# Transposing attention's probabilities, mLSTM rows and keys from copies of the rounded 32-bit type

## The chip, the cores and the metric

The kernel runs on one core of a Trainium2 chip. The time is device microseconds of one launch. The engines are named TensorE (PE in the profile, PEld for its weight loads), VectorE (DVE), ScalarE (ACT), GpSimd (POOL) and SyncE (SP, which issues nearly all DMAs).

## The reference

One layer of a hybrid backbone over 1024 latent tokens and 256 context tokens, model width 1024. Cut to what matters here:

```python
u = modulate(rmsnorm(x)) @ w_in          # split: mLSTM q,k,v,o; gates; attention q,k,v
y_m = mlstm_merge(mlstm_bidirectional(...))                 # 4 heads x 128 -> 512 columns
# attention: 8 query heads, 2 key heads, width 64, window 128, all context keys, a sink per head
s_band = einsum('bnqhgd,bnkhd->bnhgqk', qb, kb)             # masked to |i-j| <= 128
s_ctx  = einsum('bnqhgd,bchd->bnhgqc', qb, k_ctx)
p = softmax(concatenate([s_band, s_ctx, s_sink], -1))
y_a = einsum('bnhgqk,bnkhd->bnqhgd', p[band], vb) + einsum('bnhgqc,bchd->bnqhgd', p[ctx], v_ctx)
x = x + g_a * (concatenate([y_m, y_a], -1) @ w_out)
x = x + g_f * conv_glu(modulate(rmsnorm(x)))                # d_ff 2816
return rmsnorm(x) * final_norm
```

## The kernel before

Tokens lie on the 128 partitions in blocks: 2 of context, 8 of latents. Large products are made in a rounded 32-bit type (F32R, fp32r in the profile): an operand is split into a rounded part ("hi", on ScalarE) and the remainder ("lo", on VectorE), and three products are added in PSUM (`mm3`: hi*hi, hi*lo, lo*hi, lines 307 to 309).

The stages in order of time: modulation and input projection, the four mLSTM heads (to about 350 us), the query projection (to about 398 us), attention together with the first half of the output projection (to about 580 us), its second half with the norm of the mixer, the channel mixer's up product, its down product with the final norm. All that is changed lies in the query projection and attention.

In the query projection (`qgen`, `qproj`, `qtrans`) 16 query blocks are projected; each is rounded, transposed (L878, from tiles of the rounded type with the rounded identity `identr`), copied out of PSUM by ScalarE into `QTo` (L880) and stored by SP to `q_d` in HBM (L881). Between them `kprep` loads the keys of a token block (`kb`), transposes them per key head (L852) and splits them into `kT2`.

In attention a *pair* is two query heads of one query block; there are 32 pairs, four for each of the 8 blocks. A loop over steps `t` is a software pipeline: in step t pair t (`A`) gets its scores and exponentials, pair t-1 (`B`) is scaled, pair t-2 (`C`) is transposed and split, pair t-3 (`E`) finishes its product with the values; `N` is the pair after `A`. The scores of a head lie in PSUM (`sps`); `mxo` is the row maximum on VectorE (L1128), `ex` the exponential on ScalarE with the row sum in `ss` (L1132), `nrm` the reciprocal on VectorE (L1136) and the scaling in place on GpSimd (L1139). `tr(i)` transposes two key blocks of both heads from `p_` into PSUM (L1151): 512 keys make 8 transposes and 640 keys 10 for a pair, in blocks of four, four and two. `hi` (ScalarE, L1158) and `lo` (VectorE, L1164) split what comes out, and `pv` (L1174) multiplies with the values into `u`.

`Wout(b, 0)` is the mLSTM half of the output projection of block b: `load` fetches x, `tr` transposes the mLSTM rows from `ym` (L1061), `hi` and `lo` split (L1074, L1078), `mm` multiplies (L307 to L309) and `add` adds to x (L1089). Its pieces are put between those of the pairs by the table `more`, which is keyed by step and slot; block 0 (`w0`) is written into step 0 by hand.

On TensorE, VectorE, ScalarE and GpSimd the order in attention is the order in which the code is written. SP's order is made by a scheduler. Each engine and SP's queue take their instructions in order, and a DMA that waits holds up the DMAs behind it on SP.

Of the kernel before, what the change touches and what calls it, by code (L numbers as in the profile page):

```python
# [9 lines left out]
F32 = mybir.dt.float32  # L10
F32R = mybir.dt.float32r
BF16 = mybir.dt.bfloat16
AF = mybir.ActivationFunctionType
ALU = mybir.AluOpType
# [4 lines left out]
P = 128  # L19
# [10 lines left out]
KVH = 2  # L30
ADH = 64
# [47 lines left out]
def build(tc, I, out, dbg=None):  # L79
    nc = tc.nc  # L80
    dbg = dbg or {}
    V, S, G, T = nc.vector, nc.scalar, nc.gpsimd, nc.tensor
# [3 lines left out]
    ident = cp.tile([P, P], F32, name="ident")  # L86
    identr = cp.tile([P, P], F32R, name="identr")
# [24 lines left out]
    kv_d = kvp.tile([NCH, P, 2 * P], F32, name="kv_d")  # L112
# [11 lines left out]
    ym = rp.tile([P, NL, 512], F32, name="ym")  # L124
# [57 lines left out]
    xp = p1.enter_context(tc.tile_pool(name="xp", bufs=2))  # L182
# [660 lines left out]
        return row_d[8 * i:8 * i + 8, :].rearrange("(o a) b -> o (a b)", o=1).broadcast_to([P, D])  # L843

    def kprep(c):
        kb = xp.tile([P, KVH, 2, ADH], F32, name="kb", tag="kv", bufs=3)
        for i in range(2):
            nc.sync.dma_start(kb[:, :, i], kv_d[c][:, 0:P].rearrange("p (g e) -> p g e", g=KVH))
        yield
        pt = pO.tile([P, 512], F32, name="po", tag="o") if c % 2 else pU.tile([P, 2 * P], F32, name="u", tag="u")  # L850
        for g in range(KVH):
            T.transpose(pt[:, g * P:(g + 1) * P], kb[:, g].rearrange("p a e -> p (a e)"), ident[:])  # L852
        pv = pt[:, 0:256].rearrange("p (g s) -> p g s", g=KVH)
        hi, lo = (kT2[i][:, :, c * P:(c + 1) * P] for i in range(2))
        S.copy(hi, pv)
        V.tensor_tensor(out=lo, in0=pv, in1=hi.bitcast(F32), op=ALU.subtract)
# [61 lines left out]
    def load_q(b):  # L918
        QTs[b] = wm.tile([P, AH, P], F32R, name="QT", tag="QT", bufs=2)
        return nc.sync.dma_start(QTs[b][:].bitcast(F32), q_d[b]).ins  # L920
# [51 lines left out]
    for h in range(H):  # L972
# [20 lines left out]
        with tc.manual_schedule(engines=order_):  # L993
            dn = dense(h + 1, wkq, wvo, *nh) if nh else qgen()
            rate = RATE if nh else RATE3
            for n, _ in enumerate(mlstm(h, *cur)):
# [4 lines left out]
                if nh and n in (2, LW):  # L1001
                    w = wnext((n // LW,))
# [10 lines left out]
                while debt > 0:  # L1013
                    w = next(dn, None)
# [36 lines left out]
    t2 = pa_.enter_context(tc.tile_pool(name="t2", bufs=2))  # L1051


    class Wout:
        def __init__(self, b, attn):
            self.b, self.attn, self.k0, self.po = b, attn, 4 * attn, None

        def tr(self):
            self.po = pO.tile([P, 512], F32, name="po", tag="o")
            for j in range(4):  # L1060
                T.transpose(self.po[:, j * P:(j + 1) * P], ym[:, self.b, j * P:(j + 1) * P], ident[:])  # L1061

        def load(self):
            b = self.b
            self.xb = t3.tile([P, D], F32, name="x2", tag="x2") if self.attn else x2t()
            if self.attn:
                xs[b] = self.xb[:]
            nc.sync.dma_start(self.xb[:], x2_d[b][:] if self.attn else I["x"][b * P:(b + 1) * P, :])

        def hi(self):  # L1070
            self.h, self.l = (t2.tile([P, 512], F32R, name=n, tag=n, bufs=1) for n in ("ymh", "yml"))
            r = lambda a: a[:].rearrange("p (j q) -> p j q", j=4)
            self.src = yTa[:, :, self.b * P:self.b * P + P] if self.attn else r(self.po)
            S.copy(r(self.h), self.src)  # L1074
# [18 lines left out]
    class Pair:  # L1093
        def __init__(self, b, g, r):
            self.b, self.g, self.r = b, g, r
            self.lb, self.hb = max(b - 1, 0), min(b + 1, NL - 1)
            self.nb = self.hb - self.lb + 1
            self.nk = CTX + self.nb * P
            self.nkb = 2 + self.nb
            self.h0 = 4 * g + 2 * r  # L1100
            self.nm, self.ss = (t2.tile([P, 2], F32, name=n, tag=n, bufs=4) for n in ("nm2", "ss"))
            self.sps, self.p, self.sv, self.pt, self.ph, self.pl = [None] * 2, [None] * 2, [None] * 2, [None] * 3, [None] * 3, [None] * 3


        def sk(self, j):
# [26 lines left out]
            S.activation(self.p[j][:, :self.nk + 1], self.sv[j], AF.Exp, bias=self.nm[:, j:j + 1], scale=1.0,  # L1132
                         accum_out=self.ss[:, j:j + 1])

        def nrm(self):
            V.reciprocal(self.ss[:], self.ss[:])  # L1136
            for j in range(2):
                w = slice(0, self.nk)
                G.tensor_scalar(out=self.p[j][:, w], in0=self.p[j][:, w], scalar1=self.ss[:, j:j + 1],  # L1139
                                scalar2=1.0, op0=ALU.mult, op1=ALU.mult)  # L1140

        def kr(self, i):
            return range(2 * i, min(2 * i + 2, self.nkb))
# [1 line left out]
        def tr(self, i):  # L1145
            if not self.kr(i):
                return
            self.pt[i] = pT.tile([P, 512], F32, name="pt", tag="l")
            for kk, kb in enumerate(self.kr(i)):
                for j in range(2):  # L1150
                    T.transpose(self.pt[i][:, (2 * kk + j) * P:(2 * kk + j + 1) * P], self.p[j][:, kb * P:(kb + 1) * P],  # L1151
                                ident[:])

        def hi(self, i):
            w = len(self.kr(i)) * 2 * P
# [44 lines left out]
    more = collections.defaultdict(list)  # L1200

    def token(w, t):
        more[t, 1] += [w.load, w.tr]
        more[t, 2] += [w.hi]
        more[t + 1, 3] += [w.lo]
        tail_of(w, t)
# [33 lines left out]
    for t in range(n + 2):  # L1240
        blk, sub = divmod(t, 4)
        if sub == 0 and blk + 1 < NL:
            lq = load_q(blk + 1)
        if t in WOT:
            k = 4 + WOT.index(t)
            room = [wop.tile([P, D], F32R, name=f"wo{n}{k}")[:] for n in "hl"]
            with tc.issue_after(lq):
                wogs.append(load_wo(k, lambda room=room: room, G, True))
                next(wogs[-1])
        if t + 1 < len(pairs):  # L1250
            live[t + 1] = Pair(*pairs[t + 1])
        N, A, B, C, E = (live.get(t + 1 - i, null) for i in range(5))
        A.S(0)
        E.lo(2)
        B.nrm()
        fill(t, 3)
        rows_step()
        if t == 0:
            next(qpend.pop(0), 0)
            w0.tr()  # L1260
            pdk.close()
            pSs.append((pa_.enter_context(tc.tile_pool(name="pS", bufs=1, space=PSUM, side="right")), "s"))
            live[0].sk(1)
            w0.hi()
            live[0].S(1)
            w0.lo()
        E.pv(1)
        C.tr(0)
        E.pv(2)
        A.mxo(0)  # L1270
        C.hi(0)
        E.y1()
        A.ex(0)
        N.sk(0)
        C.lo(0)
        E.y2()
        fill(t, 0)
        if t == 0:
            for q in qpend:
                next(q, 0)  # L1280
        C.tr(1)
        if t:
            A.S(1)
        C.hi(1)
        A.mxo(1)
        fill(t, 1)
        C.tr(2)
        C.lo(1)
        A.ex(1)
        N.sk(1)  # L1290
        C.hi(2)
        fill(t, 2)
        C.pv(0)
        live.pop(t - 3, None)
# [253 lines left out]
    def wsplit(R, n, eng=V):  # L1548
# [29 lines left out]
                                                                    tag={"a": "a", "f": "b", "b": "b"}.get(n, "c"))  # L1578
# [105 lines left out]
    B = Block(0, None, None)  # L1684
# [21 lines left out]
    for i in range(1, NF):  # L1706
# [12 lines left out]
        if i == 1:  # L1719
# [21 lines left out]
            B = C  # L1741
# [35 lines left out]
        B = C  # L1777
# [5 lines left out]
    g = ExitStack()  # L1783
# [92 lines left out]
    more = {}  # L1876
# [87 lines left out]
    for t, (p, ps, fresh) in enumerate(products):  # L1964
        for j in range(NP):
# [35 lines left out]
            if NP + 3 <= n < NP + 3 + NL:  # L2001
                b = n - NP - 3
# [118 lines left out]
```

## Time and profile before

| | |
|---|---|
| median of 3 runs | 1279.54 us (1278.59 to 1282.48) |
| the profiled execution | span 1281.0 us from the first to the last instruction; the list of times does not say which of the three it is |
| TensorE busy | 1240.8 us, 97% |
| VectorE, ScalarE, GpSimd busy | 974.5, 638.1, 208.8 us |
| mean granted TensorE clock | 0.996 |
| DMA | 175.63 MB, 137 GB/s |

How to read the rows: a timeline row is the start in us, the duration, the engine, the line, the operation, the tiles out and in, the form, and in brackets how long the engine had been idle and what ended that. A row of the windows view is the stretch, then busy time and instructions of PE, PEld, DVE, ACT and POOL, the granted clock, the DMA engines' busy share and GB/s. With a filter by line it holds the engines that this line uses. A row of the DMA view is the transfer, the queue, how many, KB of each and the median time from issue to landing. A matmul's duration reaches from its start to the modelled end of its results, so matmuls in a row overlap.

### The profile page before, as it was taken

Reading aid. Unit: us, or ns where it says so; the run is one execution under the profiler, and the core shown is the slowest. Engines: PE = TensorE matmul, PEld = TensorE weight load, DVE = VectorE, ACT = ScalarE, POOL = GpSimd, SP = SyncE. Lnnn points to the kernel's source line nnn. Section 1 sums busy time; section 2 is a strip of 40 time slices with the busy share of each in tenths; the row PEclk is TensorE's granted clock in tenths of the full one; section 3 lists DMA queues with packets and bytes.
Section 4 is the critical chain, followed back from the end, with each engine's and each line's share of the span. In section 5 each row is a group of like instructions: output and inputs, shape, how many; then the busy total and the mean of one; then the engine's idle time right before and its main releaser. Section 6 shows DMA issues by size and latency. Waiting matters only on the chain.

```text
span 1281.0 us, 19212 instructions
## 1 busy us (share of the span) xinstructions
PE 1240.8 (97%) x7023; PEld 1060.6 (83%) x7023; DVE 974.5 (76%) x1679; ACT 638.1 (50%) x1308; POOL 208.8 (16%) x175
## 2 busy tenths in 40 slices
PE   6999999999999999999899999999999999999997
PEld 4799898999898888887677888888888888788886
DVE  5863687877887878776898777777777776867887
ACT  6632556464865777776644333333333334444435
POOL 1200000000001433232402311332321332001000
PEclk9999999999999999999999999999999999999999
DMA  9431544452254332103413222233222337975563
GB/s 361 180 122 35 141 137 143 123 168 77 84 183 162 134 116 67 67 34 132 135 63 110 105 99 95 104 119 108 101 100 99 106 108 261 345 264 172 194 199 135
DMA packets 90416, 175.63 MB, mean 137 GB/s; under 512 B 12938, under 2 KB 29522, under 8 KB 90322
## 3 DMA queue, kind: packets, MB, share of 16 engines
q1 hardware_dynamic: 90034, 173.63, 40.2%
q8 instruction: 55, 0.90, 0.3%
q10 hardware_dynamic: 288, 0.79, 0.2%
q14 instruction: 39, 0.32, 0.1%
HBM read 136.05 MB, written 38.33 MB: 136 GB/s over the span
## 4 chain that ended last, share of the span: by engine, by line
PE 78%; DVE 8%; ACT 5%; DMA 5%; issue 3%; POOL 1%; SPq 0%; DVEq 0%; ACTq 0%; POOLq 0%
PE pd L1958 14%; PE pa L1450 9%; PE pc L1450 9%; PE pp L588 6%; PE pe L1450 4%; PE pb L1450 4%; PE pd L1450 4%; PE u L1174 3%; PE pt L1151 2%; PE po L307 2%; PE pv L307 2%; PE pv L309 2%; PE pv L308 2%; PE po L309 2%; PE po L308 2%
## 5 line engine op out<-in xcount | busy, mean ns | idle before, releaser
L1552 ACT CAST wh<-Rb 128x1024 fp32r<-128x1024 f32 (+1 forms) x66 | 59.5, 903 | 147.7 <-PE pd L1450 83.0
L1958 PE MATMUL pd<-dh,al 128*128 128x512 f32 x296 | 115.4, 390 | 0.7 <-DVE al L1324 0.6
L1958 PE MATMUL pd<-dl,ah 128*128 128x512 f32 x296 | 115.2, 389 | 0.0
L1958 PE MATMUL pd<-dh,ah 128*128 128x512 f32 x296 | 115.2, 389 | 0.0
L1450 PE MATMUL pc<-hB,wh 128*128 128x512 f32 x344 | 107.1, 393 | 2.5 <-DVE av L1529 2.5
L1450 PE MATMUL pa<-hB,wh 128*128 128x512 f32 x336 | 103.6, 390 | 0.0
L1340 DVE TENSOR_TENSOR wl<-Rb,wh 128x1024 fp32r<-128x1024 f32 (+1 forms) x66 | 68.9, 1045 | 39.4 <-ACT wh L1552 38.8
L1660 POOL TENSOR_TENSOR tt<-vt,tt 128x512 f32<-128x512 f32 x22 | 29.5, 1341 | 325.6 <-ACT tt L1654 325.6
L588 PE MATMUL pp<-hl,wh 128*128 128x512 f32 x256 | 79.3, 405 | 0.0
L1450 PEld LDWEIGHTS pc<-hB,wh 128*128 128x128 f32 x344 | 65.3, 190 | 16.6 <-DVE av L1529 2.9
L307 PE MATMUL pv<-wh,hl 128*128 128x256 f32 x256 | 76.1, 297 | 0.5 <-ACT ym L601 0.5
L1450 PEld LDWEIGHTS pa<-hB,wh 128*128 128x128 f32 x336 | 63.2, 188 | 13.6 <-ACT sn L1624 0.4
L309 PE MATMUL pv<-wh,hl 128*128 128x256 f32 x256 | 72.3, 283 | 0.0
L308 PE MATMUL pv<-wl,hl 128*128 128x256 f32 x256 | 72.3, 282 | 0.0
L1450 PE MATMUL pc<-hB,wl 128*128 128x512 f32 x172 | 67.6, 393 | 0.0
L1958 PEld LDWEIGHTS pd<-dh,al 128*128 128x128 f32 x296 | 55.5, 188 | 12.8 <-DVE al L1324 1.4
L1958 PEld LDWEIGHTS pd<-dl,ah 128*128 128x128 f32 x296 | 55.6, 188 | 11.9 <-DVE dl L1324 0.3
L1450 PE MATMUL pa<-hB,wl 128*128 128x512 f32 x168 | 65.4, 389 | 0.0
L1958 PEld LDWEIGHTS pd<-dh,ah 128*128 128x128 f32 x296 | 55.6, 188 | 11.5
L1158 ACT CAST ph<-pt 128x512 fp32r<-128x512 f32 (+1 forms) x88 | 46.2, 525 | 27.0 <-PE pt L1151 26.8
L1139 POOL TENSOR_SCALAR p__4966<-p__4966,ss 128x512 f32<-128x512 f32 x1 | 0.7, 688 | 346.6 <-DVE ss L1136 346.6
L1450 PE MATMUL pe<-hB,wh 128*128 128x512 f32 x176 | 54.6, 390 | 0.4 <-DVE hB L1340 0.2
(1072 smaller groups left out, 3760.2 us busy)
## 6 DMA issues: line engine op xcount, KB each, us to landing
w<-in_w_ada_dram SPq DMA_DIRECT2D x64, 256.0 KB, 2.7
br<-in_w_down_dram SPq DMA_DIRECT2D x25, 512.0 KB, 6.6
Ra<-in_w_up_dram SPq DMA_DIRECT2D x22, 512.0 KB, 3.6
Rb<-in_w_up_dram SPq DMA_DIRECT2D x22, 512.0 KB, 3.5
ar<-act_s SPq DMA_DIRECT2D x44, 256.0 KB, 3.6
act_a<-tt SPq DMA_DIRECT2D x33, 256.0 KB, 2.0
act_s<-tt SPq DMA_DIRECT2D x33, 256.0 KB, 2.0
wr<-in_w_h_dram SPq DMA_DIRECT2D x16, 512.0 KB, 4.4
```

The costliest lines, as they stand in the source:

```text
L307: T.matmul(ps, st_hi, mv_hi, start=first, stop=False)
L308: T.matmul(ps, st_hi, mv_lo, start=False, stop=False)
L309: T.matmul(ps, st_lo, mv_hi, start=False, stop=last)
L588: T.matmul(pp[:, 512 * n:512 * n + 512], wkq[sw][:, kt, cs], hl[n][part][:, kt, :], start=kt == 0 and sw + part == 0, stop=kt == KT - 1 an ...
L1151: T.transpose(self.pt[i][:, (2 * kk + j) * P:(2 * kk + j + 1) * P], self.p[j][:, kb * P:(kb + 1) * P], ident[:])
L1158: S.copy(self.ph[i][:, :w], self.pt[i][:, :w])
L1174: T.matmul(self.u[:], vv[:, c, self.g], part[i][:, kk * 2 * P:(kk + 1) * 2 * P], start=kb + m == 0, stop=kb == last and m == 1)
L1340: sub = lambda e, o, x, y: e.tensor_tensor(out=o, in0=x, in1=y, op=ALU.subtract)
L1450: T.matmul(ps[:], wt[sw][:, j, ks], hB[part][:, blk, kt, :], start=first and kt == 0 and sw + part == 0, stop=last and kt == 3 and sw == 1 ...
L1552: S.copy(wt[0][:], src)
L1660: G.tensor_tensor(out=self.tt[:, h2_], in0=self.vt[:], in1=self.tt[:, h2_], op=ALU.mult)
L1958: T.matmul(ps[:], ac[sa][:, js], w[sw], start=first and n == 0, stop=last and n == 2, skip_group_check=not fresh)
```

## The change

Three kinds of transposes take their input from a tile of type F32R, with the rounded identity, and write a PSUM tile that is viewed as F32R. The input tile is filled by a DMA whose destination is viewed as plain F32, so the bits are those of the plain numbers.

- Keys: `kb` is of type F32R; the loads that filled it before now fill it under a view as F32.
- mLSTM rows: `Wout.load` also copies the block's rows from `ym` (SBUF) into a new tile `ymb` (SBUF, 256 KB, two buffers), and `tr` reads that. In `token` the load of a block moves from slot 1 of step t, just ahead of its transposes, to slot 2 of step t-1.
- Probabilities: `nrm` takes one head at a time. After the scaling a DMA on SP copies the head's probabilities from `p_` into a new tile `pq_` (256 or 320 KB, five buffers), and `tr` reads that. The first head's `nrm` comes behind its pair's second exponential (`A.nrm(0)`), the second's where both were (`B.nrm(1)`).

```diff
-        kb = xp.tile([P, KVH, 2, ADH], F32, name="kb", tag="kv", bufs=3)
+        kb = xp.tile([P, KVH, 2, ADH], F32R, name="kb", tag="kv", bufs=3)
         for i in range(2):
-            nc.sync.dma_start(kb[:, :, i], kv_d[c][:, 0:P].rearrange("p (g e) -> p g e", g=KVH))
+            nc.sync.dma_start(kb[:, :, i].bitcast(F32), kv_d[c][:, 0:P].rearrange("p (g e) -> p g e", g=KVH))
...
-            T.transpose(pt[:, g * P:(g + 1) * P], kb[:, g].rearrange("p a e -> p (a e)"), ident[:])
+            T.transpose(pt[:, g * P:(g + 1) * P].bitcast(F32R), kb[:, g].rearrange("p a e -> p (a e)"), identr[:])
...
-                T.transpose(self.po[:, j * P:(j + 1) * P], ym[:, self.b, j * P:(j + 1) * P], ident[:])
+                T.transpose(self.po[:, j * P:(j + 1) * P].bitcast(F32R), self.yb[:, j * P:(j + 1) * P], identr[:])
...
+            if not self.attn:
+                self.yb = t2.tile([P, 512], F32R, name="ymb", tag="ymb", bufs=2)
+                nc.sync.dma_start(self.yb[:].bitcast(F32), ym[:, b])
...
-        def nrm(self):
-            V.reciprocal(self.ss[:], self.ss[:])
-            for j in range(2):
-                w = slice(0, self.nk)
-                G.tensor_scalar(out=self.p[j][:, w], in0=self.p[j][:, w], scalar1=self.ss[:, j:j + 1],
-                                scalar2=1.0, op0=ALU.mult, op1=ALU.mult)
+        def nrm(self, j):
+            w = slice(0, self.nk)
+            V.reciprocal(self.ss[:, j:j + 1], self.ss[:, j:j + 1])
+            G.tensor_scalar(out=self.p[j][:, w], in0=self.p[j][:, w], scalar1=self.ss[:, j:j + 1],
+                            scalar2=1.0, op0=ALU.mult, op1=ALU.mult)
+            self.q[j] = t2.tile([P, 640], F32R, name="pq_", tag="pq_", bufs=5)
+            nc.sync.dma_start(self.q[j][:, w].bitcast(F32), self.p[j][:, w])
...
-                    T.transpose(self.pt[i][:, (2 * kk + j) * P:(2 * kk + j + 1) * P], self.p[j][:, kb * P:(kb + 1) * P],
-                                ident[:])
+                    T.transpose(self.pt[i][:, (2 * kk + j) * P:(2 * kk + j + 1) * P].bitcast(F32R),
+                                self.q[j][:, kb * P:(kb + 1) * P], identr[:])
...
     def token(w, t):
-        more[t, 1] += [w.load, w.tr]
+        more[t - 1, 2] += [w.load]
+        more[t, 1] += [w.tr]
...
         E.lo(2)
-        B.nrm()
+        B.nrm(1)
...
         A.ex(1)
+        A.nrm(0)
```

SP's order at the border of the query projection and attention, before. `QT` is the load of a query block, `q_d<-QTo` the stores of the query projection, the first `x` the load of `w0`, the second that of block 1.

```order
L920 DMA QT<-q_d 128x1024
L881 DMA q_d<-QTo 128x512 x3
L1068 DMA x_4926<-in_x_dram 128x1024
L881 DMA q_d<-QTo 128x512 x2
L1068 DMA x_5074<-in_x_dram 128x1024
L881 DMA q_d<-QTo 128x512
L1091 DMA x_d_75<-x_4926 128x1024
```

The same place after the change (lines behind the edits are counted on by 3 to 6).

```order
L920 DMA QT<-q_d 128x1024
L881 DMA q_d<-QTo 128x512 x3
L1068 DMA x_4926<-in_x_dram 128x1024
L881 DMA q_d<-QTo 128x512
L1071 DMA ymb<-ym 128x512
L881 DMA q_d<-QTo 128x512
L1068 DMA x_5048<-in_x_dram 128x1024
L1071 DMA ymb<-ym 128x512 x2
L881 DMA q_d<-QTo 128x512
L1144 DMA pq__4999<-p__4968 128x512
L1144 DMA pq__5019<-p__4995 128x512
L1094 DMA x_d_75<-x_4926 128x1024
```

`w0`'s copy of the mLSTM rows stands behind its x and the fourth of the six stores; on TensorE its transposes keep their place, right behind the last-but-one block of query transposes.

VectorE around the border of two steps in the middle (the row maximum and the reciprocals are those of pair 6), before: `nm` is the row maximum, `pl` a remainder, `yTa` the attention output, `yml` the remainder of the mLSTM rows.

```order
L1128 TENSOR_REDUCE nm_5233<-sps 128x1
L1164 TENSOR_TENSOR pl__5372<-pt,ph 128x512
L1164 TENSOR_TENSOR pl__5396<-pt,ph 128x256
L1136 RECIPROCAL ss<-ss 128x2
L1078 TENSOR_TENSOR yml<-po,ymh 128x512
```

And after:

```order
L1131 TENSOR_REDUCE nm_5261<-sps 128x1
L1168 TENSOR_TENSOR pl__5408<-pt,ph 128x512
L1140 RECIPROCAL ss<-ss 128x1
L1168 TENSOR_TENSOR pl__5436<-pt,ph 128x256
L1140 RECIPROCAL ss<-ss 128x1
L1081 TENSOR_TENSOR yml<-po,ymh 128x512
```

The reciprocal of a pair is split: the first head's stands ahead of the third remainder, the second's where both were. In the first steps, which have no third remainder yet, the two stand next to each other.

The scheduler also moves the load of `er` (the first weights of the channel mixer) on SP from behind a store of x that follows the last query load to behind the query load of block 6, and with it ScalarE's rounding of `er` from ahead of pair 27's first exponential to ahead of pair 20's.

More of the change, by code (lines that the diff above doesn't have):

```diff
@@ L1101, in __init__ @@
             self.nm, self.ss = (t2.tile([P, 2], F32, name=n, tag=n, bufs=4) for n in ("nm2", "ss"))
-            self.sps, self.p, self.sv, self.pt, self.ph, self.pl = [None] * 2, [None] * 2, [None] * 2, [None] * 3, [None] * 3, [None] * 3
+            self.sps, self.p, self.q, self.sv, self.pt, self.ph, self.pl = [None] * 2, [None] * 2, [None] * 2, [None] * 2, [None] * 3, [None] * 3, [None] * 3
         def sk(self, j):
```

## The prediction

> **What bounds the kernel now.** I read the page's first line, then the windows view over the attention stage, where every edit lies, then the TensorE timeline there, and last the queues that the new copies use.
>
> ```profile
> PE 1240.8 (97%) x7023; PEld 1060.6 (83%) x7023; DVE 974.5 (76%) x1679; ACT 638.1 (50%) x1308; POOL 208.8 (16%) x175
> 398.00:414.00 16.00, 14.30 (x95) 12.08 (x95) 9.12 (x19) 9.84 (x28) 3.27 (x5) 1.00 0.45 149
> 414.00:549.00 135.00, 133.44 (x941) 113.51 (x939) 110.63 (x220) 104.08 (x280) 50.85 (x58) 1.00 0.28 98
> 549.00:578.00 29.00, 27.16 (x186) 23.64 (x184) 21.93 (x45) 20.18 (x57) 8.13 (x12) 1.00 0.05 19
> ```
>
> TensorE is occupied for 97% of the span. In the long middle of attention, 414 to 549 us, it is occupied for 133.44 of 135 us at the full clock, with VectorE second at 110.63. So what leaves TensorE there should leave the time, less what new waits take. The first 16 us and the last 29 us are different: there TensorE idles 1.7 and 1.8 us, and a late input moves everything behind it.
>
> **The change part by part. First, the transposes.** Their number comes from the windows view filtered by line, one row each for the probabilities (L1151), the mLSTM rows (L1061) and the keys (L852):
>
> ```profile
> 352.00:585.00 233.00, 47.03 (x304) 36.08 (x304) 1.00 0.31 107
> 352.00:585.00 233.00, 4.87 (x32) 3.36 (x32) 1.00 0.31 107
> 352.00:585.00 233.00, 4.05 (x20) 2.07 (x20) 1.00 0.31 107
> ```
>
> The duration in such a row, about 273 ns, is not the price: matmuls overlap. The price is the time from one start to the next. The kernel already transposes from a tile of the rounded type at one place, the query heads (L878), so both kinds can be read from the timeline. Each pair of pieces below goes from the first transpose of a block to the second 256-wide matmul behind it.
>
> ```profile
> 394.04 0.46 PE L878 MATMUL pt<-identr,qs 128*128 128x128 f32 x4
> 394.33 0.35 PE L307 MATMUL px<-wh,hl 128*128 128x256 f32 x1
> 394.52 0.28 PE L308 MATMUL px<-wl,hl 128*128 128x256 f32 x1
> ...
> 434.87 0.27 PE L1151 MATMUL pt<-ident,p__5260 128*128 128x128 f32 x1
> 434.98 0.27 PE L1151 MATMUL pt<-ident,p__5291 128*128 128x128 f32 x1
> ...
> 435.43 0.28 PE L1118 MATMUL sps<-kT,QT 128*128 128x256 f32 x1
> ```
>
> Four rounded transposes and one 256-wide matmul take 394.52 - 394.04 = 0.48 us; four plain ones and the same matmul take 435.43 - 434.87 = 0.56 us. A block of four saves 0.08 us. It is the first transposes that gain; at the end the matmul behind starts late in both cases.
>
> ```profile
> 358.27 0.89 PE L878 MATMUL pt<-identr,qs 128*128 128x128 f32 x8
> 359.19 0.28 PE L308 MATMUL px<-wl,hl 128*128 128x256 f32 x1
> ...
> 429.42 0.27 PE L1151 MATMUL pt<-ident,p__5193 128*128 128x128 f32 x1
> ...
> 430.41 0.28 PE L1118 MATMUL sps<-kT,QT 128*128 128x256 f32 x1
> ```
>
> A block of eight saves (430.41 - 429.42) - (359.19 - 358.27) = 0.07 us. The 304 of the probabilities stand in 56 blocks of four, 4 of eight and 24 of two; two are nowhere timed in the rounded kind, so between nothing and half a block of four, 0.02 taken: 56 x 0.08 + 4 x 0.07 + 24 x 0.02 = 5.3 us. The mLSTM rows are 8 blocks of four; the first stands in the front of the stage, below, so 7 x 0.08 = 0.6. The keys are 10 blocks of two next to rounded transposes: 0.2. Together at most 6.1 us of TensorE.
>
> How much of it counts? In places TensorE is already waiting for the chain transpose, ScalarE's rounding, VectorE's remainder, product. The idle rows show two such waits in the middle, and the timeline shows small ones as late starts:
>
> ```profile
> PE pt L1151 <- DVE pl__6393 L1164: 0.6, 1, 0.6
> ...
> 434.29 0.36 PE L1174 MATMUL u<-ph,vv 128*128 128x256 f32 x1
> 434.64 0.39 PE L1174 MATMUL u<-pl__5396,vv 128*128 128x256 f32 x1
> ...
> L1136 DVE RECIPROCAL ss<-ss 128x2 f32<-128x2 f32 x32 | 5.0, 157 | 1.4 <-ACT p__4993 L1132 0.8 <-ACT p__7331 L1132 0.2 <-ACT p__5148 L1132 0.2
> ```
>
> At such a place a transpose that ends sooner only lengthens the wait. VectorE, which does the remainder, also gets 32 more reciprocals of up to 157 ns (at most 5.0 us in all), one of them now ahead of the third remainder in every step. It has 24 us free in the middle, so I give them no term, but that cover goes where the remainder is waited for. Of the 6.1 us I take 60%, 3.7; the ends are 0 and 6.1. GpSimd's 64 scalings stay the same in number and size.
>
> **Second, the copies of the mLSTM rows.** Seven of the eight are issued a step ahead. The first cannot be: on SP it now stands behind the query store that waits for ScalarE's rounding of the fourteenth of the sixteen query blocks, while its transposes are the next thing on TensorE.
>
> ```profile
> 397.47 0.33 SPq L1068 DMA_DIRECT2D x<-in_x_dram  x1
> 398.65 0.32 SPq L881 DMA_DIRECT2D q_d<-QTo  x1
> ...
> 398.74 0.62 PE L1061 MATMUL po<-ident,ym 128*128 128x128 f32 x4
> 400.00 0.39 PE L1117 MATMUL sps<-kT,QT 128*128 128x256 f32 x1 [0.64 <-ACT sps L1108]
> 401.24 0.51 PE L307 MATMUL po<-woh,ymh 128*128 128x512 f32 x1 [0.44 <-DVE yml L1078]
> ...
> q_d<-QTo SPq DMA_DIRECT2D x3, 256.0 KB, 2.8
> act_a<-tt SPq DMA_DIRECT2D x33, 256.0 KB, 2.0
> x<-in_x_dram SPq DMA_DIRECT2D x8, 512.0 KB, 3.6
> ```
>
> The store is issued at 398.65 and takes 0.32 to issue, so the copy starts at about 399.0. No row shows a copy inside SBUF. The nearest are the stores of the same 256 KB from SBUF, 2.0 us where the engines are quiet and 2.8 in this window; a 512 KB load takes 3.6, which is the upper end, and nothing excludes a quicker landing than 2.0 but no row has one. With 2.4 it lands at 401.4 instead of being there at 398.74: TensorE's transpose is 2.7 us late. Behind it wait the rounding, the remainder (401.24 follows 398.74 by 2.5 us, all of it chain) and the first output products, and the score matmul at 400.00 with its own 0.64 us of waiting is behind it in order too. VectorE's row maxima stand behind that remainder, so nothing later catches up: +2.7 us, between 2.0 and 4.0.
>
> The Trainium skill, "DMA: Bandwidth & Descriptors", section on the anatomy of one DMA, fits a transfer as a fixed 2.0 us plus its bytes at 436 GB/s, mostly the wait for the write's receipt; it measured GpSimd's path. It speaks against this change, since each new copy would pay that latency whatever its size. By it, as an estimate, 256 KB take 2.6 us and the front is 2.9 us late instead of 2.7; the 2.0 us row for 256 KB is under it.
>
> **Third, the 64 copies of the probabilities.** Each needs GpSimd's scaling before and its transposes after. The old distance is the cover:
>
> ```profile
> 411.13 0.69 POOL L1139 TENSOR_SCALAR p__5033<-p__5033,ss 128x512 f32<-128x512 f32 x1
> 413.71 0.27 PE L1151 MATMUL pt<-ident,p__5033 128*128 128x128 f32 x1
> ...
> 440.17 1.05 POOL L1139 TENSOR_SCALAR p__5421<-p__5421,ss 128x640 f32<-128x640 f32 x1 [2.48 <-DVE ss L1136]
> 444.96 0.27 PE L1151 MATMUL pt<-ident,p__5421 128*128 128x128 f32 x1
> ...
> 563.87 0.69 POOL L1139 TENSOR_SCALAR p__7166<-p__7166,ss 128x512 f32<-128x512 f32 x1 [5.08 <-DVE ss L1136]
> 567.73 0.27 PE L1151 MATMUL pt<-ident,p__7166 128*128 128x128 f32 x1
> ```
>
> From the fifth pair on the first head is scaled in the step before, so the second takes its place on GpSimd: it ends at about 441.2 for a transpose at 444.96, 3.7 us ahead, and at 564.6 for 567.73, 3.2 us ahead, the narrowest. A copy of 2.0 to 2.8 us plus 0.3 for the issue fits. In the first pairs the reciprocals still stand together, and pair 1's second head ends at 411.82 for 413.71: 1.9 us of cover, 0.4 to 1.2 short. Pair 0 is short by 0 to 0.4. I take 0.8 for both. SP is not full: 72 more issues of 0.33 us in 180 us. Behind a copy that waits for GpSimd stand only the loads of later steps. The load of er moves forward, so ScalarE's rounding of it (about 1 us) lands in the step of pair 20 instead of pair 27: 0 to 1 us if er is late, 0.2 taken.
>
> **Sum.** -3.7 + 2.7 + 0.8 + 0.2 = 0.0 against the profiled execution's span of 1281.0 us, which is 1.5 us over the median of the runs. I predict the median unchanged: 1279.5 us. Its own range is -3 to +3, 1276.5 to 1282.5. A measurement of this kernel tells about 0.3%, 3.8 us, from no change.
>
> **Rivals.** *The gain comes whole* (faster): TensorE has no idle in the middle worth naming, which speaks for it; the late starts above speak against. With all 6.1 us and the lower ends of the waits, 2.0 + 0.3: -3.8, or 1275.7; with the front copy hidden too, -5.8, 1273.7. *The copies come late in the middle* (slower): decided when issue plus landing pass 3.2 to 3.8 us, the cover in most steps. The 3.6 us of loads, and loads of 512 KB in the same rings, speak for it; the 2.0 of stores against. At 4.2 us about 20 steps would wait 0.5 us, once each: with the front 1.3 us later still, -3.7 + 4.0 + 0.8 + 0.2 + 10 = +11, 1291. *Nothing is saved in the middle*: between products the loading of the next weights shows, and the chain over ScalarE and VectorE sets the pace. Then 2.7 + 0.8 + 0.2 = +3.7, 1283.2, on the edge of what is told.
>
> **How the numbers follow.** Forecast 0.54, gain whole 0.20, late copies 0.12, nothing saved 0.14. From the second, three quarters are faster by over 0.3%, and a tenth of the forecast: 0.21. From the third nearly all and half of the last are slower, with little of the first: 0.20. Within: 0.59. The range goes from 1274.5, which leaves out a third of the whole gain, to 1284.0, which leaves out the late copies: about 2 in 10 outside.
>
> **What would show it.** L1155's starts 85 ns apart or less inside a block (now 109 or 110); the first L1061 near 401.4 with a DMA as releaser, and no gain before 414; in the windows view 414 to 549 shortened by 3 to 4 us; no rows of PE waiting for pq past the second pair. Wrong would be: pq in the list of waits in every step, er's rounding waited for, or the product rows waiting for the remainder longer by as much as the transposes gave.

## The result and the profile after

The changed kernel is slower: 1287.84 us median of 4 runs (1287.09 to 1290.82) against 1280.66 of the kernel before beside it (1278.59 to 1282.48), a ratio of 1.0064 with a 95% interval of 1.005 to 1.0078. That is 7.2 us more. The forecast was 1279.5, no change, with a range that ended at 1284.0. It was wrong: the kernel is slower than that whole range. The profiled execution took 1287.09 us, with a span of 1285.3. Among all the runs below, one execution (the profiled one of e9) took 2022.66 us at a granted clock of 0.558, and no ratio counts it.

The page of the changed kernel, TensorE's line, and the windows view over the same three stretches as in the prediction (the program runs up to 8.5 us later here):

```profile
PE 1238.9 (96%) x7023; PEld 1057.4 (82%) x7023; DVE 976.2 (76%) x1711; ACT 638.4 (50%) x1308; POOL 210.0 (16%) x175
398.00:414.00 16.00, 11.52 (x51) 9.36 (x51) 4.88 (x10) 5.04 (x15) 1.39 (x2) 0.79 0.53 190
414.00:549.00 135.00, 128.59 (x917) 108.35 (x916) 111.84 (x241) 102.08 (x276) 50.55 (x58) 0.99 0.61 222
549.00:578.00 29.00, 27.63 (x204) 23.98 (x203) 23.37 (x53) 22.50 (x62) 8.04 (x11) 1.00 0.41 158
```

TensorE has as many instructions as before, and is busy 1.9 us less. But in 398 to 414 us it gets through 51 matmuls where it did 95, and the column after the five engines, the granted clock, reads 0.79 where it was 1.00. In the middle the DMA engines are busy 0.61 of the time, against 0.28.

The waits view of TensorE over 396 to 590 us names who ended the idle time. None of the rows for DMA or for `pl__6610` was there before; the two 0.8 rows were 0.6.

```profile
PE po L1061 <- DMA ymb<-ym: 3.9, 1, 3.9
PE pt L1155 <- DMA pq__5044<-p__5022: 1.5, 1, 1.5
...
PE u L1178 <- DVE pl__6610 L1168: 0.9, 1, 0.9
PE pt L1155 <- DMA pq__5440<-p__5410: 0.9, 1, 0.9
PE pt L1155 <- DVE pl__6500 L1168: 0.8, 1, 0.8
...
PE pt L1155 <- DVE pl__5808 L1168: 0.8, 1, 0.8
```

The largest wait on TensorE's timeline, and what comes behind it. The rows are start, duration, engine, line, tiles, and in brackets the idle time:

```profile
397.25 0.52 PE L878 MATMUL pt<-identr,qs 128*128 128x128 f32 x4
401.70 0.72 PE L1061 MATMUL po<-identr,ymb 128*128 128x128 f32 x4 [3.93 <-DMA ymb<-ym]
...
405.26 0.63 PE L307 MATMUL po<-wrm,ymh 128*128 128x512 f32 x1
405.69 0.63 PE L308 MATMUL po<-wrm,ymh 128*128 128x512 f32 x1
...
408.06 0.39 PE L308 MATMUL po<-wrm,ymh 128*128 128x512 f32 x1
408.30 0.39 PE L309 MATMUL po<-wrm,yml 128*128 128x512 f32 x1
```

The wait itself is 3.93 us. Then 512-wide matmuls follow each other at 0.43 us (405.26 to 405.69) where the full clock gives 0.24 (408.06 to 408.30): TensorE came out of the idle time at half its clock, which the trace records from 400.99 to 407.82. The prediction had no such term. The Trainium skill, "TensorE: Matmul & The Clock Gate", section "What's actually happening", says that the clock falls to half after at least one idle window of about 3.4 us. The trace agrees here: the wait is longer than that, and the clock is half behind it. But in some of the runs below a wait of about 2 us was enough, which is shorter than what the Trainium skill states; the runs decide, and e11 has their numbers.

SP's timeline for the copies that were late, and the DMA view's times from issue to landing (last column) for pairs 0 and 1:

```profile
397.52 0.32 SPq L881 DMA_DIRECT2D q_d<-QTo  x1
398.00 0.53 SPq L1071 DMA_DIRECT2D ymb<-ym  x1
...
414.46 0.33 SPq L1094 DMA_DIRECT2D x_d<-x  x1
415.32 0.47 SPq L1144 DMA_DIRECT2D pq__5044<-p__5022  x1
416.00 1.14 SPq L1144 DMA_DIRECT2D pq__5061<-p__5040  x1
```

```profile
pq__4999<-p__4968 SPq DMA_DIRECT2D x1, 256.0 KB, 2.3
...
pq__5044<-p__5022 SPq DMA_DIRECT2D x1, 256.0 KB, 4.2
pq__5061<-p__5040 SPq DMA_DIRECT2D x1, 256.0 KB, 4.2
```

A copy of 256 KB inside SBUF lands after 2.3 us for pair 0. Block 0's rows, issued at 398.00, were used at 401.70: 3.7 us. Pair 1's copies took 4.2.

All the kernels issue the same 7023 matmuls in the same order (e2's 34 extra ones are left out), so the start of each one can be subtracted. The table has what that difference grows by in each stretch of attention (times are those of the kernel before), for the profiled execution of each kernel, in us. "Rest" adds up the three stretches between the named ones. The experiments follow below.

| kernel | front 384.1-413.5 | pair 1 413.5-423.9 | pair 6 439.4-441.2 | er 512.3-512.6 | rest to 573.4 | sum |
|---|---|---|---|---|---|---|
| changed kernel | +5.47 | +3.34 | +0.86 | +1.12 | -2.74 | +8.05 |
| e1 block 0 plain | -0.05 | +3.59 | +1.08 | +1.28 | -2.97 | +2.92 |
| e2 TensorE kept busy | +3.45 | +0.77 | +1.08 | +1.27 | -2.10 | +4.47 |
| e3 block 0, pairs 0, 1 plain | -0.07 | +0.46 | +1.33 | +1.27 | -3.23 | -0.24 |
| e4 no copies | -0.09 | -0.22 | -0.05 | +0.02 | -1.25 | -1.58 |
| e5 er back | +5.11 | +3.38 | +1.26 | +0.01 | -2.86 | +6.90 |
| e6 as e3, er back | -0.10 | +0.75 | +1.11 | +0.02 | -2.82 | -1.04 |
| e7 copies, plain type | +4.35 | +5.30 | +1.23 | +1.19 | -0.69 | +11.38 |
| e8 no copies, er back | -0.09 | -0.24 | -0.05 | +0.04 | -2.72 | -3.07 |
| e9b block 0, pairs 0, 1, 2, 6 plain, er back | -0.02 | +1.02 | +0.02 | +0.05 | -2.63 | -1.55 |
| e10 copy on GpSimd's queue | +7.75 | +3.41 | +1.41 | +1.25 | -3.10 | +10.72 |
| e11 block 0 plain, store moved | -0.09 | +1.75 | -0.05 | +1.22 | -1.24 | +1.58 |

Two differences lie outside these stretches. The query projection ends 0.5 to 1.0 us sooner in 10 of the 12 profiles. Most of it is a wait of 0.62 us for `kb` at 384.11 in the profile of the kernel before; e7, whose keys are plain, lacks that wait too, so it isn't the type's. And the profile of the kernel before loses time of its own at 690 to 705 us:

```profile
696.36 0.73 PE L1450 MATMUL pc<-hB,wh 128*128 128x512 f32 x2 [2.49 <-DVE av L1529]
...
697.44:700.85 3.41, 3.41 (x10) 2.65 (x9) 3.02 (x4) 1.33 (x2) 0.00 (x0) 0.50 0.48 154
```

TensorE waits 2.49 us for `av`, where the changed kernel waits 1.14, and the clock behind it is half. That is 3.0 us, so the two profiled spans differ by 4.3 us only; the 7.2 us are the difference of the medians.

### The profile page after: what moved, and what is told of

The parts are those of the page before. It is cut to its first block, busy times and chain, and to the rows that moved or that the text cites. A ratio compares the mean times of both kernels' runs of the same rounds, so it can differ in the third digit from the quotient of the medians.

```text
span 1285.3 us, 19452 instructions
## 1 busy us (share of the span) xinstructions
PE 1238.9 (96%) x7023; PEld 1057.4 (82%) x7023; DVE 976.2 (76%) x1711; ACT 638.4 (50%) x1308; POOL 210.0 (16%) x175
## 4 chain that ended last, share of the span: by engine, by line
PE 79%; DVE 8%; ACT 5%; DMA 4%; issue 3%; POOL 1%; SPq 0%; DVEq 0%; ACTq 0%; POOLq 0%
PE pd L1964 14%; PE pa L1456 9%; PE pc L1456 8%; PE pp L588 6%; PE pe L1456 4%; PE pb L1456 4%; PE pd L1456 4%; PE po L307 2%; PE u L1178 2%; PE pv L307 2%; PE pv L309 2%; PE pv L308 2%; PE po L309 2%; PE po L308 2%; PE px L309 1%
## 5 line engine op out<-in xcount | busy, mean ns | idle before, releaser
L1131 DVE TENSOR_REDUCE nm<-sps 128x1 f32<-128x641 f32 (+1 forms) x64 | 50.3, 786 | 6.2 <-PE sps L1127 4.7
```

Source lines behind the costliest of these rows:

```text
L1131: V.tensor_reduce(out=self.nm[:, j:j + 1], in_=self.sv[j], axis=AX.X, op=ALU.max, negate=True)
```

## The experiments

Times are medians; each ratio is to the kernel before, run on the same chip (1280.14 to 1280.84 us), with its 95% interval.

**e1: block 0's rows plain.**

```diff
-                T.transpose(self.po[...].bitcast(F32R), self.yb[...], identr[:])
+                if self.b == 0:
+                    T.transpose(self.po[...], ym[:, 0, j * P:(j + 1) * P], ident[:])
+                else: ...   # as before, and load() copies only where b > 0
```

> The changed kernel, with block 0's mLSTM rows alone transposed plain, straight from ym, and not copied. Theory T1: the loss of 7.2 us is two waits for copies in the crowded start (3.9 us for the rows of block 0 at L1061, 1.5 + 0.3 us for pair 1's probabilities at L1155), and behind each wait a stretch at half the TensorE clock (6.8 us and 3.4 us, which cost about 2 and 1.5 us); the rest of the kernel gains 1 to 3 us. T1 expects here no wait for ymb at block 0 and a full clock from 401 to 410 us: 5 to 6 us less than the changed kernel, 1 to 2.5 us more than the kernel before (1281.5 to 283 against 1280.7, so 1281.7 to 1283.2). Rival R1: the half clock behind the wait has nothing to do with the wait: it stays, and 3 to 4 us are won. Rival R2: the copies late in the middle and their traffic are the loss: at most 3 us are won, and the kernel stays 4 us or more behind the kernel before.

Measured: 1283.51 us, ratio 1.0023 (1.0014 to 1.0032). The wait for `ymb` is gone, the front costs nothing (-0.05 in the table), the clock in 398 to 414 us is 1.00. The waits view and the window of pair 1:

```profile
PE pt L1158 <- DMA pq__5042<-p__5020: 1.7, 1, 1.7
414.00:437.00 23.00, 20.52 (x136) 17.18 (x135) 16.15 (x36) 14.72 (x42) 8.80 (x10) 0.93 0.73 260
```

Pair 1's wait stays, with a half clock of its own behind it (0.93 in the window). R1 and R2 fall: one copy, the first, made about 4 us of the 7.2, where T1 had 5 to 6.

**e2: the same wait, but TensorE kept busy.**

```diff
             self.po = pO.tile([P, 512], F32, name="po", tag="o")
+            if self.b == 0:
+                for _ in range(34):
+                    T.transpose(self.po[:, 0:P], ident[:], ident[:])
```

> The changed kernel with 34 transposes of the identity put ahead of block 0's four row transposes, so that TensorE works through the wait for the copy of block 0's rows (about 34 x 0.11 = 3.7 us of work) and the wait itself stays. Theory T1 (an idle TensorE is what brings the half clock): the row transposes start as late as in the changed kernel, but the clock stays full from 401 to 410 us and about 2 us are won: 1285.0 to 1286.3 us. Rival R1 (the half clock there has another cause, such as the load of the chip at that place): the half clock stays at the same place and the time stays within 1 us of the changed kernel's 1287.8.

Measured: 1283.63 us, ratio 1.0026 (1.0015 to 1.0038): 4.2 us won, where T1 had 2. Window and TensorE's timeline:

```profile
398.00:414.00 16.00, 14.55 (x104) 12.62 (x104) 6.64 (x16) 6.69 (x19) 1.97 (x3) 1.00 0.61 198
398.45 3.90 PE L1062 MATMUL po<-ident 128*128 128x128 f32 x34
402.55 0.51 PE L1064 MATMUL po<-identr,ymb 128*128 128x128 f32 x4 [0.19 <-DMA ymb<-ym]
...
405.03 0.40 PE L309 MATMUL po<-woh,yml 128*128 128x512 f32 x1
405.26 0.39 PE L307 MATMUL po<-wrm,ymh 128*128 128x512 f32 x1
```

The row transposes are as late as in the changed kernel, 4.1 us behind the last query transposes, and the clock stays full: 0.23 us from one 512-wide matmul to the next. So it is TensorE's idleness that brings the half clock, and the half clock is 5.47 - 3.45 = 2.0 us of the front. The rest of the win is at pair 1, whose copies landed after 2.4 us in this profile, with 0.2 us of wait. What sets these quick copies apart is taken up under e11.

**e3: pairs 0 and 1 plain too.**

```diff
+            if 4 * self.b + 2 * self.g + self.r < 2:
+                return                      # nrm: no copy; tr reads p_ with ident
```

> The changed kernel, with block 0's mLSTM rows and the probabilities of the first two pairs transposed plain and not copied. Theory T1: both front waits and both half-clock stretches go, and what is left is the middle's own gain of 1 to 3 us: 1277.7 to 1280.5 us, below the kernel before (1280.7). Rival R2 (late copies and traffic in the middle): no less than 1283 us. Rival R3 (the lateness moves on: pairs 2 and 3, whose copies are now the first in the same crowded stretch, wait in the place of pair 1): 1281 to 1283 us with a new wait of 1 us or more on the copies of pair 2 or 3.

Measured: 1281.32 us, ratio 1.0007 (0.9998 to 1.0016): 2.2 us less than e1, all full clock, and still not below the kernel before. Two of the waits that the prediction had at nothing or nearly so are left, pair 6 (1.33 in the table) and er (1.27). So T1 was too kind to the middle. The time lies in R3's range, but R3's new wait on pair 2 or 3 is only 0.3 us.

**e4: the type without the copies.** GpSimd scales straight into the rounded tile, and block 0's rows are plain. The kernel leaves out the low bits of the probabilities, so it prices the type and is no replacement.

```diff
-            G.tensor_scalar(out=self.p[j][:, w], in0=self.p[j][:, w], ...)
-            nc.sync.dma_start(self.q[j][:, w].bitcast(F32), self.p[j][:, w])
+            G.tensor_scalar(out=self.q[j][:, w], in0=self.p[j][:, w], ...)
```

> As the first of these (block 0's rows plain), and GpSimd scales the probabilities straight into the rounded tile, so that no DMA copies them; the low bits of the probabilities are left out. It prices the type without the copies of probabilities. Theory T1: TensorE's saving in the middle shows without any wait for a copy: 3 to 5 us below the kernel before (1275.7 to 1277.7 us). Rival R4 (the type itself saves nothing on the path, the waits on VectorE and GpSimd take it all): within 1 us of the kernel before.

Measured: 1280.94 us, ratio 1.0004 (0.9994 to 1.0014). With no copy of probabilities at all, the gain that T1 expected does not show. The timeline of ScalarE, VectorE and TensorE near 508 us says why:

```profile
507.11 1.05 ACT L1331 CAST e0h<-er 128x1024 fp32r<-128x1024 f32 x1 [1.23 <-DMA er<-in_w_up_dram]
508.19 1.22 DVE L1332 TENSOR_TENSOR e0l<-er,e0h 128x1024 fp32r<-128x1024 f32 x1 [1.20 <-ACT e0h L1331]
509.49 0.38 PE L1180 MATMUL u<-ph,vv 128*128 128x256 f32 x1 [1.47 <-ACT ph L1164]
```

ScalarE stands 1.23 us for the load of er, rounds for 1.05, and the probabilities' own rounding `ph` is behind it in order. This is the moved step to which the prediction gave 0.2 us. In the table it stands under "rest" here. The time alone would fit R4; the next four runs take the moved step and the type apart.

**e5: er's load held back to its old place.**

```diff
+    with tc.issue_after(x_stored[6]):      # the store of block 6's x
         nc.sync.dma_start(er[:], ...)
```

> The changed kernel, with the load of er held on SP until behind the store of block 6's x, as it stands before the change; ScalarE's and VectorE's rounding of er follow it back to pair 27's step. Theory T1 with what the first four runs added (the earlier rounding of er stops TensorE for 1.1 to 1.6 us in every one of them, of which the old place cost about 0.4): 0.7 to 1.2 us less than the changed kernel's 1287.8, so 1286.6 to 1287.1 us, and the wait of TensorE at the product rows near 510 us gone. Rival (the old place costs as much, so that er's place makes no difference): within 0.5 us of 1287.8 with a wait of 1 us or more at 550 us.

Measured: 1287.9 us, ratio 1.0054 (1.0041 to 1.0067). In the trace the step at 512 us goes from +1.12 to +0.01, and a wait of 0.5 us stands at the old place. The time that T1 expected did not come, and in the time this run alone settles nothing, since its interval overlaps the changed kernel's. The pairs with a clean front do better: e3 to e6, and e4 to e8.

**e6: block 0, pairs 0 and 1 plain, and er held back** (e3 and e5 together).

> Block 0's mLSTM rows and the first two pairs transposed plain and not copied, and er's load held back as in the run beside it. T1: all that was lost in the front and at er is gone, and what is left is the middle's gain of about 2.9 us less 1.4 at pair 6's copy: 1279.0 to 1280.5 us, 0 to 1.5 below the kernel before. Rival (what is gained at one place is given back at the next chain of transpose, rounding, remainder, product): 1281 us or more, no better than with er early (1281.3).

Measured: 1279.78 us, ratio 0.9997 (0.9988 to 1.0006): 1.5 us under e3, level with the kernel before. What is left over is 0.75 at pairs 1 and 2 and 1.11 at pair 6.

**e7: all the copies, the plain type.**

```diff
-            self.q[j] = t2.tile([P, 640], F32R, name="pq_", tag="pq_", bufs=5)
+            self.q[j] = t2.tile([P, 640], F32, name="pq_", tag="pq_", bufs=5)
...   # the same for kb and ymb; the three transposes with ident
```

> The changed kernel with all its copies and its order, but the three copied or loaded tiles of the plain type and the transposes plain: the copies without the type. T1: the type's own gain, about 2.9 us in the middle and 0.5 in the keys, is lost and the waits stay: 1290.0 to 1291.5 us. Rival (the type itself saves nothing on the path): within 1 us of the changed kernel's 1287.8. Rival (the half clock behind the waits comes from the rounded type's matmuls and not from the idleness): the half clock goes and the time is 1287 or less.

Measured: 1290.72 us, ratio 1.0077 (1.0064 to 1.009), 2.9 us above the changed kernel, though the two intervals overlap a little, and 2.0 us of the profile's difference are at pair 1, where the half clock lasts longer. The table's "rest" says it better: -0.69 with the plain type and -2.74 with the rounded one, so 2.1 us are the type's. The half clock comes here too. That the reciprocals are split costs nothing: before er, the plain type's stretches change by -0.00 and -0.15 us.

**e8: no copies, er held back** (e4 and e5 together).

> As the run in which GpSimd scales straight into the rounded tile (low bits of the probabilities left out, block 0's rows plain), with er's load held back. T1: the type's gain of 2.9 us in attention shows nearly whole, less about 0.4 at er's old place: 1277.5 to 1279.8 us, 0.5 to 2.5 below the kernel before. Rival (nothing saved on the path): 1280 to 1281 us.

Measured: 1278.46 us, ratio 0.9984 (0.9975 to 0.9992): 1.7 us faster than the kernel before, and 2.5 less than e4 (1.5 less in the table), more than er's step was thought to cost. The trace has -3.07 us over attention: this is all that the type is worth here. Like e4, the kernel leaves out the low bits of the probabilities.

**e9 and e9b: copies only where the old distance covers them.** Block 0 and pairs 0, 1, 2 and 6 plain, er held back. e9b is the same kernel, run again for its trace.

```diff
-            if 4 * self.b + 2 * self.g + self.r < 2:
+            if 4 * self.b + 2 * self.g + self.r in (0, 1, 2, 6):
```

> Block 0's mLSTM rows and the probabilities of pairs 0, 1, 2 and 6 transposed plain and not copied, the other 28 pairs and 7 blocks as in the changed kernel, er's load held back: copies only where the old distance covers them. T1: the waits left in the run with pairs 0 and 1 plain (0.8 us at pair 2, 1.1 at pair 6) go, the blocks of these two pairs save nothing (about 0.2): 1.5 us below that run's 1279.8, so 1277.8 to 1278.8 us, 1.3 to 2.3 below the kernel before. Rival (the lateness moves to the next copies in the same crowded stretches, pair 3 and pair 7): 1279.5 us or more and a wait of 0.5 us or more on one of them.

> The version with copies only where the old distance covers them (block 0's rows and pairs 0, 1, 2 and 6 plain, er's load held back), for its trace. T1: no wait of TensorE for a copy above 0.5 us between 396 and 590 us, the full clock there, and 1277.8 to 1279.5 us. Rival: pair 3's or pair 7's copies are waited for in the place of those taken out.

Measured: 1278.92 us, ratio 0.9983 (0.9973 to 0.9994), and 1278.76 us, ratio 0.998 (0.9969 to 0.999). This version beats both kernels: 1.9 us (0.2%) under the kernel before, 9 under the changed one. Its waits for copies:

```profile
PE pt L1166 <- DMA pq__5157<-p__5126: 0.4, 1, 0.4
...
PE pt L1166 <- DMA pq__5185<-p__5153: 0.3, 1, 0.3
```

T1 holds, but for 0.1 us in the time of e9, and the rival in small: pair 3's copies are now the first in the crowded stretch and are waited for, 0.7 us in all.

**e10: block 0's copy from GpSimd's queue.**

```diff
-                nc.sync.dma_start(self.yb[:].bitcast(F32), ym[:, b])
+                (nc.sync if b else nc.gpsimd).dma_start(self.yb[:].bitcast(F32), ym[:, b])
```

> The changed kernel, with the copy of block 0's mLSTM rows issued from GpSimd's queue, which has nothing in it there, instead of SP's, where it stands behind the query stores. Theory T1 (the first wait is the late issue behind SP's stores plus a crowded landing): the copy starts before 398.0 us and the wait of 3.9 us shrinks or goes; if it goes, with it the half clock behind it, and the time is that of the run with block 0 plain, 1283 to 1284.5 us. Rival (the copy waits for its tile's memory, which the query projection frees only at its end, or lands late wherever it is issued): a wait of 2 us or more stays and the time stays above 1286 us.

Measured: 1290.98 us, ratio 1.0078 (1.0062 to 1.0094). T1 falls, and the rival's wait and time came. GpSimd's timeline, the wait, and the landing in the DMA view:

```profile
399.81 0.74 POOL L1071 DMA_DIRECT2D ymb<-ym  x1 [339.67 <-ACT QTo L880]
PE po L1061 <- DMA ymb<-ym: 6.3, 1, 6.3
ymb<-ym POOLq DMA_DIRECT2D x1, 256.0 KB, 5.5
```

On an empty queue the copy still waits, for ScalarE's write of `QTo` in the query projection. The trace names the releaser, not the reason; the copy's tile comes from a pool that is opened behind the projection, and that it takes over memory used there is the likely reason, not one shown. Whatever holds it, taking the copy out of SP's order did not let it start sooner. It also landed later, after 5.5 us against 3.7 on SP's queue. That is one copy each, and on SP's queue copies of the mLSTM rows of later blocks took up to 6.1 us (e6), so the queue isn't shown to be the reason.

**e11: the 512 KB store behind pair 1's copies** (e1, with one store moved).

```diff
+            if (self.b, self.g, self.r, j) == (0, 0, 1, 1):
+                with tc.issue_after(cp):     # cp: pair 1's second copy
+                    nc.sync.dma_start(x2_d[0][:], w0.xb[:])
```

> As the run with block 0's rows plain (1283.5 us), with one store moved: block 0's x, 512 KB, which SP issued 0.9 us ahead of pair 1's two copies, is issued right behind them. Theory T1 (the copies land after 4.2 to 4.4 us there, and not after 2.3 as pair 0's do, because they run beside that store): the copies of pair 1 land after 2.3 to 2.6 us, TensorE's wait of 1.7 us there and the half clock behind it go: 1280.0 to 1281.5 us. Rival (they land late for another reason, such as the first copy's tiles or the order of the rings): the landing stays at 4 us or more, and the time within 1 us of 1283.5.

Measured: 1281.99 us, ratio 1.0008 (0.9996 to 1.0019), 1.5 us under e1. SP's timeline, the wait, the window:

```profile
409.94 0.47 SPq L1148 DMA_DIRECT2D pq__5041<-p__5020  x1
410.62 0.46 SPq L1148 DMA_DIRECT2D pq__5058<-p__5037  x1
411.17 0.54 SPq L1151 DMA_DIRECT2D x_d<-x  x1
PE pt L1162 <- DMA pq__5058<-p__5037: 2.0, 1, 2.0
414.00:437.00 23.00, 21.72 (x158) 18.55 (x159) 17.83 (x39) 17.61 (x48) 9.79 (x11) 1.00 0.82 290
```

The first copy landed sooner (no wait for it), the second did not: the store now stands 0.55 us behind it and it still came 2.0 us late. T1 is half right at best, and the store ahead of these copies isn't alone what makes them late: in e2 it stands there too, and both copies are quick. One row of the DMA view tells the cases apart. The first row here stands beside the one of SP's queue (q1) in the changed kernel, from the issue of pair 1's first copy to the landing of its second; for the same stretch in e2 the second row is all there is:

```profile
q8 instruction: 1, 0.02, 1.1%
...
q1 hardware_dynamic: 509, 1.19, 99.4%
```

In each of the six profiles in which a copy of pair 1 is late (the changed kernel, e1, e5, e7, e10, e11) a packet of 16 KB of the kind "instruction" runs on the DMA engines while these copies do; in e2, where both land after 2.4 us, none does. No run moves that packet alone, so that it delays the copies is likely, not shown.

A wait of 2.0 us was followed by no half clock this time, though 1.75 and 0.33 us in e1 were, and 2.05 in e5. The traces record each change of the clock, and within attention all of them lie a whole number of steps of 3.41 us apart. These are the steps around pair 1's wait, two of the changed kernel and two of e11 (counted back from its next change, at 642.62):

```profile
418.06:421.47 3.41, 1.56 (x15) 1.33 (x14) 1.41 (x3) 0.91 (x3) 1.13 (x2) 1.00 0.86 302
421.47:424.88 3.41, 3.41 (x12) 2.85 (x12) 2.65 (x7) 2.74 (x9) 0.54 (x1) 0.50 0.93 323
...
410.52:413.93 3.41, 2.16 (x15) 1.67 (x14) 2.56 (x7) 2.29 (x8) 1.44 (x3) 1.00 0.80 300
413.93:417.34 3.41, 2.50 (x18) 2.23 (x19) 1.61 (x5) 1.92 (x6) 0.00 (x0) 1.00 0.54 178
```

In the changed kernel 1.85 of the 3.41 us are idle in one step, and the next is at half clock. In e11 the longer wait is cut by the border of a step, 1.25 and 0.91 us are idle, and the clock stays full. From 30 to 1265 us of the 13 profiles (the two kernels and all runs but e9), every full-clock step with 1.85 us or more of idle time was followed by half clock (15 of 15), and none with less than 1.3 us; between the two it went both ways. So the cost of a wait of about 2 us depends on where it falls in these steps, and that differs from profile to profile.

## Why the prediction was wrong, step by step

- **TensorE's saving, 6.1 at most, 3.7 taken.** The pieces were sized rightly: over the 56 blocks of four the median is 0.071 us less, over those of eight 0.10, of two 0.02. One block of the changed kernel: 476.91 to 477.40 is 0.49 us, forecast 0.48. The starts inside a block are 65 ns apart in the median, three in four of them within the 85 that the prediction named.

```profile
476.91 0.22 PE L1155 MATMUL pt<-identr,pq__5839 128*128 128x128 f32 x1
...
477.21 0.35 PE L1120 MATMUL sps<-kT,QT 128*128 128x256 f32 x1
477.40 0.28 PE L1121 MATMUL sps<-kT,QT 128*128 128x256 f32 x1
```

  (The sum itself has a slip: 56 x 0.08 + 4 x 0.07 + 24 x 0.02 is 5.2, not 5.3.) The share that counts was too high: 2.7 us in the rest of attention and 3.1 in all of it without waits for copies (e8), 2.1 as the difference of types (e7), a third to a half instead of 60%. The waits for VectorE's remainder took part of it, as argued (0.6 to 0.8 us in two rows). The idea behind it holds.
- **The first mLSTM copy, 2.7 taken, bounds 2.0 to 4.0.** The place and the wait were right, the landing was 3.7 us instead of 2.4, within the bounds, and TensorE was 3.3 us late behind it (4.05 at L1061, 0.74 made up by the score matmul's old wait). What failed is "nothing later catches up: +2.7": it took lateness as the whole cost. The half clock added 2.2 us, so the term was 5.5. This is the larger of the failed steps. The estimate of 2.6 us for 256 KB by the Trainium skill, "DMA: Bandwidth & Descriptors" (section on the anatomy of one DMA), stood in the prediction too: pair 0's 2.3 is near it, the 3.7 here and pair 1's 4.2 are not.
- **Pairs 0 and 1, 0.8 taken.** Pair 0 was not late (2.3 us). Pair 1, for which 1.2 us was the upper end, waited 1.87 us, since its copies took 4.2 us, beyond the 2.8 of the stores in that window; half clock made it 3.3. No row of the prediction gives the 4.2: its slowest, loads of 512 KB, is 3.6, and in e2 the same copies beside the same store took 2.4. The issue was short too: 0.47 us for a copy, not 0.3.
- **The middle hidden.** Right for nearly all: TensorE waits 0.9 us for pair 6 and 0.3 for one more. Pair 6's second copy is issued between two 512 KB loads, at 3.7 us of cover, and took 4.5:

```profile
442.71 0.58 SPq L1359 DMA_DIRECT2D x<-x_d  x1
443.39 0.47 SPq L1144 DMA_DIRECT2D pq__5440<-p__5410  x1
443.95 0.54 SPq L920 DMA_DIRECT2D QT<-q_d  x1
...
pq__5440<-p__5410 SPq DMA_DIRECT2D x1, 320.0 KB, 4.5
```

  The rival "late in the middle" had the right mechanism and 20 steps; here it was one, and a second in small. Which copy is late can change: in e11 another, at 468 us, was waited for for 1.2 us.
- **er, 0.2 taken, 0 to 1.** The place (pair 20) was right, the price 1.1 to 1.3 at that place, of which 0.5 leaves the old one (e5). ScalarE's rounding alone was costed; VectorE's 1.2 us of remainder was not, and the wait that stands there in the changed kernel is for VectorE (`pl__6610`, 0.9). The prediction had named a wait for er's rounding as a sign of being wrong; this wait stands behind it.
- **Sum.** -2.7 + 5.5 + 3.3 + 0.9 + 1.1 = +8.1 in the trace, less 0.9 in the query projection: +7.2. That it equals the difference of the medians is partly luck, since the profiled spans differ by 4.3 (the kernel before loses 3.0 at 690 to 705 us in its profile). Of the forecast's error, 2.8 is at the first copy, 2.5 at pair 1, 1.0 in the gain, and 1.8 at pair 6 and er, less the projection's 0.9.

## What to carry to other kernels

Before a copy is put into a chain, look for the places where its consumer comes next on the bound engine: in steady state the old distance hid nearly all of it here, and the loss came from the first steps and from a step beside large loads. There allow for a late landing (3.7 to 4.5 us here), not the quickest (2.3). A wait of TensorE of two to four microseconds may cost one and a half to two more, since the clock can stay at half for 3.4 to 6.8 us behind it; where a wait can't be avoided, work that nobody needs costs less than idling (e2, 4.2 us). A scheduler may answer new tiles and copies by moving a load and its rounding into a place where they have a price (er): read the order for what the diff doesn't name.

## What the runs showed that I had not expected

- TensorE's clock fell to half behind idle times of 3.8 to 6.3 us in every run that had one, and stayed full with the same wait filled with 34 transposes that nothing uses (0.79 against 1.00 granted). Idle times of about 2 us brought it where 1.8 us or more fell into one step of 3.41 us, and not where the border of a step cut them (e11); one of 1.35 us (pair 6 in e3) did not.
- A copy inside SBUF of 256 KB took 2.3 us at best. Pair 1's took 4.2 to 4.5 in six profiles and 2.4 in e2, with the same 512 KB store 0.9 us ahead in most of them; the six have a 16 KB instruction packet beside the copies, e2 has none.
- Block 0's copy, issued from GpSimd's queue, took 5.5 us, but SP's queue has copies that were as slow.
